# Products of the conditioning vectors with w_mod: steps of two column groups become steps of four

## The chip, the cores and the metric

The kernel runs on one core of a Trainium2 chip. A core has a matrix engine (TensorE, PE in the profile, with its weight loads as PEld), VectorE (DVE), ScalarE (ACT), GpSimd (POOL) and SyncE (SP), which issues this kernel's DMAs. The metric is the device time of one execution in microseconds; the median of several runs counts.

## The reference

One inference step of a two-layer decoder trunk, for a prompt of 1024 positions and 8 samples of 4 positions (1056 rows of width 1024). Layer 0 mixes tokens with sliding-window attention, layer 1 with a gated delta rule. Ahead of each layer the rows are normalised and modulated, and behind it the branch is gated, by vectors made from a conditioning vector c (one for the prompt, eight for the samples):

```python
def modulate(x, c, norm_g, w_mod, b_mod):
    shift, scale, gate = jnp.split(jax.nn.silu(c) @ w_mod + b_mod, 3, axis=-1)
    h = rms_norm(x, norm_g) * (1 + scale[:, None]) + shift[:, None]
    return h, gate[:, None]
...
    for layer in range(DEPTH):
        hp, gp = modulate(xp, c_prompt, norm_g[layer], w_mod[layer], b_mod[layer])
        hs, gs = modulate(xs, c_sample, norm_g[layer], w_mod[layer], b_mod[layer])
...
        xp = xp + gp * op
        xs = xs + gs * osm
```

`w_mod` is 1024 x 3072 float32 for each layer: 1024 columns of shift, 1024 of scale, 1024 of gate. All 9 conditioning vectors go through it at once.

## The kernel before

**The products.** The 9 vectors silu(c), padded to 32, lie transposed in `cT` (128 partitions, 8 row blocks, 32 columns). A product takes one row block k of `cT` as the weights of TensorE (128 x 32) and one piece of `w_mod` (128 rows by 512 columns, 256 KB) as the moving operand. Its output has 32 rows, so it uses a quarter of the array's columns; the first row of its output in the PSUM bank (0, 32, 64 or 96) says which quarter, called a column group here. Eight products, k = 0 to 7, add up to one 512-column piece of the result. Where fewer than four pieces are made in one bank, even and odd k go to different groups and are added later.

**Where they stand.** Shift and scale of layer 0 are made at the start (lines 717 to 743, `modulation_steps`) and stay as they are. Three others are touched:

1. The gate of layer 0: `modulation_gate(0)`, called at line 1218, during the projections of q and v. Two pieces j = 0, 1; step k does two products, to the groups 32 j + 64 (k mod 2). The loads go to the pool `wp`, tag "wr", which has four buffers and which the other weights use too. Loads and steps are put off by `defer(late_p, ticks, fn)` and called by `tick`, which the projections call at the fourth row block of every column group of a q projection (three times) and of every block of v (nine times, t = 0 to 8). `pin` makes the next matmul of the projection wait in program order for the step's last product. At the end VectorE adds rows 0 to 63 of the bank to `modGt`, and ScalarE copies rows 64 to 127.
2. Shift and scale of layer 1: `modulation_rest` (line 1256), beside the attention of layer 0 and its other projections. Four pieces, loaded two at a time into two buffers (tag "wm" of the pool `at`), in 16 steps i of two products each; step i waits until the tick counter of the projections has advanced 20 i (`MM = (0, 20)`), loads its two pieces and waits for them.
3. The gate of layer 1: `modulation_gate(1)`, started at line 1373 in the output projection of layer 0. `pos` counts row blocks of that projection, 16 for a block of 128 rows; step k waits for `pos` to reach 32 + 15 k (`MS`), then does its two products, each when its piece is there, and loads for k + 2, again into "wr". When all is done, `first_weights` (line 1419) loads the first weights of layer 1 into the same four buffers: `cwr`, then two halves that become `kw0h`, `kw0l`, `kw1h`, `kw1l`.

**What sets the order.** Up to line 1287 the Tile scheduler orders the work; engines take their instructions strictly in that order. From there on `Core` is the planner: it keeps a clock for every engine from prices of its own (`issued`, line 111), and generators registered by `weave` yield conditions on these clocks (`ready`, `soon`, `idle`), on ticks or on `pos`. Between two matmuls of the main loop `stages()` runs every generator whose condition holds, the lowest rank in `K` first (`cached` 9, `modulate` 31). What is written so is the program order of every compute engine. The planner prices a float32 product with 32 output rows at 2400 columns per us where its group differs from that of the matmul before it, at 600 otherwise.

Of the kernel before, what the change touches and what calls it, by code (L numbers as in the profile page):

```python
# [5 lines left out]
F32 = mybir.dt.float32  # L6
# [8 lines left out]
P = 128  # L15
D = 1024
KD = D // P
# [202 lines left out]
def body(tc, I, O, cst_ap, dbg=None):  # L220
    nc = tc.nc
# [6 lines left out]
    wp = es.enter_context(tc.tile_pool(name="wp", bufs=1, side="right"))  # L228
# [16 lines left out]
    MS = (32, 15)  # L245
    AH, AI = (a / 10 for a in AM)
    VK = ()
    MM = (0, 20)
# [15 lines left out]
    cT = cp.tile([P, KD, 32], F32, name="cT")  # L264
# [60 lines left out]
    Sc = [cp.tile([P, KD, 9], F32, name=f"Sc{l}") for l in range(2)]  # L325
    modGt = cp.tile([P, 512], F32, name="modG")

    def wmod_tile(l, k, c0):
        wt = wp.tile([P, 512], F32, tag="wr", name="wmod", bufs=4)
        nc.sync.dma_start(wt, I["w_mod"][l, k * P:(k + 1) * P, c0:c0 + 512])  # L330
        return wt

    def modulation(l, load, js=(0, 1)):


        step, end = modulation_steps(l, load, js)
        for k in range(KD):
            step(k)
        return end

    def modulation_steps(l, load, js, pm=None):
        pm = pm or psb("mi")
        nj = len(js)

        def step(k, i=None, q0=0):
            for q, wt in enumerate(load(k if i is None else i)):
                q += q0
                if nj == 1:
                    q += 2 * (k % 2)
                mm = nc.tensor.matmul(pm[32 * q:32 * q + 32, :], cT[:, k, :], wt,  # L350
                                      start=(k <= 2 - nj), stop=(k >= KD - 3 + nj), skip_group_check=True)
            return mm

        return step, lambda: modulation_end(l, js, pm)
# [27 lines left out]
                                           gT[:, l, 4 * j:4 * j + 4].unsqueeze(2).to_broadcast([P, 4, 9]),  # L382
                                           ALU.add, ALU.mult)

    def modulation_gate(l):

        for j in range(2):
            c0 = 2 * D + 512 * j
            nc.sync.dma_start(modGt[32 * j:32 * j + 32], I["b_mod"][l:l + 1, c0:c0 + 512].partition_broadcast(32))
        pg = psb("lg" if l == 0 else "tr")  # L390
        wts = {}

        def load(k):
            wts[k] = [wmod_tile(l, k, 2 * D + j * 512) for j in range(2)]

        def step(k, j):
            r0 = 32 * j + 64 * (k % 2)
            pin[:] = [nc.tensor.matmul(pg[r0:r0 + 32, :], cT[:, k, :], wts[k][j], start=(k < 2), stop=(k >= KD - 2),
                                       skip_group_check=True)]

        def end():
            nc.vector.tensor_tensor(modGt[0:64], modGt[0:64], pg[0:64, :], ALU.add)
            nc.scalar.copy(modGt[64:P], pg[64:P, :])

        if l == 0:
            return load, lambda k: (step(k, 0), step(k, 1)), end

        def steps():
            for k in range(2):
                load(k)  # L410
            for k in range(KD):
                yield lambda: pos[0] >= MS[0] + MS[1] * k
                for j in range(2):
                    yield ready(wts[k][j])
                    step(k, j)
                if k + 2 < KD:
                    load(k + 2)
            yield soon(pg)
            yield idle("vector", modGt)
            end()  # L420

        return steps()
# [42 lines left out]
    late_p, late_c, pin = [], [], []  # L465
# [5 lines left out]
    def defer(late, ticks, fn):  # L471

        late.append([ticks, fn])
# [47 lines left out]
    def ready(*ts):  # L521
        return lambda: plain() or nc.ready(ts) <= nc.free["tensor"]
# [11 lines left out]
    held, pos = {}, [0]  # L534
# [174 lines left out]
    for i, ts in enumerate(xb):  # L709
# [3 lines left out]
        mm = turn_x(ts, dgs, nxt[1])  # L713
# [20 lines left out]
    step, end = modulation_steps(0, lambda k: wm_half[1][k], (1,))  # L734
# [27 lines left out]
    at = at_guard.__enter__()  # L762
    if True:
# [451 lines left out]
        k0 = kproj(0)  # L1215
        q0 = [qproj(0, 0)]
        wv = vproj()
        load, step, end = modulation_gate(0)
        for k in range(KD):
            defer(late_p, k + 1, lambda k=k: load(k))  # L1220
            defer(late_p, k + 3, lambda k=k: step(k))
        defer(late_p, 11, end)
        q0.append(qproj(0, 1))
        hsel = wp.tile([P, P], F32, tag="wr", name="hsel", bufs=4)
        o, w = COFF["hsel"]
# [7 lines left out]
        for t in range(NB + 1):  # L1233
# [3 lines left out]
            for k in range(KD):  # L1237
                hi, lo = wv[k // 2]
                for x, y in ((hhi, hi), (hlo, hi), (hhi, lo)):
                    with pinned():  # L1240
                        mm = nc.tensor.matmul(pv, x[:, k, t * P:t * P + parts], y[:, k % 2, :],
                                              start=(n == 0), stop=(n == 23))
# [12 lines left out]

        def modulation_rest():

            def load(i):
                wts = []
                for j in range(2):  # L1260
                    wt = at.tile([P, 512], F32, tag="wm", name="wm", bufs=2)
                    c0 = (2 * (i % 2) + j) * 512
                    nc.sync.dma_start(wt, I["w_mod"][1, (i // 2) * P:(i // 2 + 1) * P, c0:c0 + 512])
                    wts.append(wt)
                return wts

            pm = yield from bank("tr")
            step, _ = modulation_steps(1, lambda i: wts, (0, 1), pm)
            for i in range(2 * KD):
                yield lambda: ticks[0] >= t0 + MM[0] + MM[1] * i  # L1270
                wts = load(i)
                yield ready(*wts)
                step(i // 2, i, 2 * (i % 2))
            yield soon(pm)
            ma = at.tile([P, 512], F32, tag="wm", name="ma", bufs=2)
# [35 lines left out]
    if True:  # L1311
# [24 lines left out]
        def add_out(pj, i, t, hf):  # L1336

            parts = P if t < NB else TS
            ns = slice(hf * 512, (hf + 1) * 512)
            yield lambda: gathered[0] == 2 * i + hf and i in rows_ and shaped[0] >= i - 1 + hf  # L1340
            xt = rows_[i][0:parts]
            if t < NB:
                yield idle("vector", pj)
                y = x2.tile([P, 512], F32, tag="y", name="y", bufs=2)
                nc.vector.tensor_tensor(y, pj, gate[:, ns], ALU.mult)
                opened.pop(0)
            else:
# [12 lines left out]
                give("lg", pg)  # L1360
            eng = "vector" if i == NB and hf else "gpsimd"
            yield idle(eng, y, xt)
            getattr(nc, eng).tensor_tensor(xt[:, ns], xt[:, ns], y[0:parts], ALU.add)
            if hf == 0:
                rows_["ss", i] = sm.tile([P, 2], F32, tag="ss", name="ss")[0:parts]
            yield soon(xt)
            nc.scalar.activation(y[0:parts], xt[:, ns], AF.Square, accum_out=rows_["ss", i][:, hf:hf + 1])
            gathered[0] += 1
            if hf == 1:
                nc.sync.dma_start(x1d[t * P:t * P + parts], xt)  # L1370
                weave(shape(i, t, xt, rows_["ss", i], parts), "shape")
                if t == NB:
                    weave(modulation_gate(1), "mod")

        def shape(i, t, xt, ss, parts):

# [59 lines left out]
        for i, t in enumerate(turned_):  # L1436
# [7 lines left out]
            for kk, hf in order if i < NB else sorted(order, key=lambda o: o[::-1]):  # L1444
                if True:
                    ns = slice(hf * 512, (hf + 1) * 512)
                    if hf not in pjs:
                        tag = ("pj", "pj", "mi", "mi")[outs[0] % 4]
# [5 lines left out]
                    for k in range(4 * kk, 4 * kk + 4):  # L1454
# [188 lines left out]
    if True:  # L1643
# [534 lines left out]
        pos, prepared, stored, opened, gathered, outs = [0], {}, [0], [], [-1], [0]  # L2178
# [485 lines left out]
    nc = nc.nc  # L2664
# [36 lines left out]
```

## Time and profile before

| | us |
|---|---|
| median of 3 runs (lowest, highest) | 1768.01 (1766.73, 1768.91) |
| the profiled execution | 1762.72 |
| its span, first to last instruction | 1760.8 |

The profile is of one execution, and its view of the busy time by stretch gives for each engine the time in which it worked. "Granted clock" is the share of TensorE's full clock that the throttle let through; its mean was 0.986. In the view by tile, a line "x64: a/b/c, s to t" has the count, the least, median and greatest duration in ns, and the first and last start in us. In the time line a row has start, duration, engine, line, operation, out<-in, shapes and a count of merged instructions; from line 1287 on, all compute instructions are issued by a helper and carry its line, L89.

### The profile page before, as it was taken

How to read it: one execution, taken by the hardware profiler on the slowest of the kernel's cores; microseconds unless marked ns; L12 is line 12 of the kernel's file. 1: busy time of each engine (PE TensorE's matmuls, PEld its weight loads, DVE VectorE, ACT ScalarE, POOL GpSimd, SP SyncE). 2: the span in 40 equal slices, each digit the busy share in tenths (PEclk: the TensorE clock that was granted, in tenths of full speed). 3: DMA queues.
4: the chain of work that ended last, by engine and by line, in shares of the span. 5: the costliest groups of instructions: out<-in, count | busy, mean ns of one | idle time of the engine just before them, and what ended most of it. 6: DMA issues, size and time to landing. Idle time of an engine off the chain costs nothing. (4 is left out here: it accounts for less than half of the span.)

```text
span 1760.8 us, 31819 instructions
## 1 busy us (share of the span) xinstructions
PE 1670.2 (95%) x10666; PEld 1450.0 (82%) x10666; DVE 1214.9 (69%) x3538; ACT 864.3 (49%) x2514; POOL 603.6 (34%) x1170
## 2 busy tenths in 40 slices
PE   6999999999998989799999999999999998998897
PEld 5988888877777889679999999899998987766685
DVE  5426676554555678867878778688697884458677
ACT  5525565453334555156554655564656564433332
POOL 2401110112122234344443544444344445323332
PEclk9999999999999999899999999999999999999999
DMA  9442121233333232132422324224133126764885
GB/s 338 131 112 61 49 69 49 67 103 110 102 108 101 62 88 61 52 87 53 115 61 70 95 62 112 60 67 120 39 94 82 45 76 187 240 193 145 265 258 168
DMA packets 281572, 191.77 MB, mean 109 GB/s; under 512 B 98361, under 2 KB 253881, under 8 KB 281378
## 3 DMA queue, kind: packets, MB, share of 16 engines
q1 hardware_dynamic: 281410, 189.75, 37.5%
q8 instruction: 84, 1.38, 0.3%
q14 instruction: 78, 0.64, 0.1%
HBM read 144.68 MB, written 47.04 MB: 109 GB/s over the span
## 5 line engine op out<-in xcount | busy, mean ns | idle before, releaser
L89 PE MATMUL ps_pj<-h2hi,wl 128*128 128x384 f32 (+1 forms) x1128 | 381.1, 338 | 2.7 <-POOL wl L89 2.5
L89 PE MATMUL ps_pj<-h2lo,wh 128*128 128x384 f32 (+1 forms) x1128 | 381.3, 338 | 0.0
L89 PE MATMUL ps_pj<-h2hi,wh 128*128 128x384 f32 (+1 forms) x1128 | 379.4, 336 | 0.6 <-ACT XR L89 0.6
L89 POOL TENSOR_TENSOR wl<-wr,wh 128x512 fp32r<-128x512 f32 x122 | 164.8, 1352 | 545.7 <-ACT wh L89 518.8
L89 PEld LDWEIGHTS ps_pj<-h2hi,wl 128*128 128x128 f32 x1128 | 213.7, 189 | 6.9 <-POOL wl L89 3.6
L89 PEld LDWEIGHTS ps_pj<-h2hi,wh 128*128 128x128 f32 x1128 | 213.5, 189 | 3.9 <-ACT XR L89 0.9
L89 PEld LDWEIGHTS ps_pj<-h2lo,wh 128*128 128x128 f32 x1128 | 213.6, 189 | 3.7
L89 POOL TENSOR_TENSOR xt<-xt,y 128x512 f32<-128x512 f32 (+1 forms) x48 | 63.3, 1323 | 176.0 <-DVE y L89 137.6
L89 PE MATMUL ps_pj<-hlo,wh 128*128 128x384 f32 (+1 forms) x360 | 119.6, 332 | 0.0
L89 PE MATMUL ps_pj<-hhi,wh 128*128 128x384 f32 (+1 forms) x360 | 118.6, 330 | 0.0
L89 PE MATMUL ps_pj<-hhi,wl 128*128 128x384 f32 (+1 forms) x360 | 118.0, 328 | 0.0
L89 DVE SCALAR_TENSOR_TENSOR vT<-XR,cT,vT 128x384 f32<-128x384 f32 (+1 forms) x144 | 90.3, 640 | 37.9 <-ACT vT L89 36.0
L89 DVE TENSOR_TENSOR tmp<-X 64x31 f32<-64x31 f32 (+15 forms) x248 | 91.2, 368 | 15.5 <-POOL X L89 12.3
L89 DVE TENSOR_TENSOR X<-X,tmp 64x31 f32<-64x31 f32 (+15 forms) x248 | 95.2, 384 | 8.5
L89 ACT CAST wh<-wr 128x512 fp32r<-128x512 f32 x122 | 75.1, 616 | 20.9 <-PE ps_pj L89 15.6
L89 PEld LDWEIGHTS ps_pj<-hlo,wh 128*128 128x128 f32 x360 | 67.8, 188 | 13.6 <-issue 13.5
L89 ACT COPY XR<-ps_pj 128x384 f32<-128x384 f32 (+1 forms) x96 | 43.2, 450 | 68.8 <-PE ps_pj L89 68.6
L89 PEld LDWEIGHTS ps_pj<-hhi,wh 128*128 128x128 f32 x360 | 67.7, 188 | 5.9 <-issue 4.2
L89 ACT ACTIVATE qe<-ps_mi,Eg 128x128 f32<-128x128 f32 x112 | 35.1, 364 | 74.4 <-PE ps_mi L89 74.4
L89 PEld LDWEIGHTS ps_pj<-hhi,wl 128*128 128x128 f32 x360 | 67.8, 188 | 3.3 <-issue 3.3
L89 ACT ACTIVATE prob<-prob,nm 128x256 f32<-128x256 f32 (+1 forms) x128 | 62.3, 489 | 11.3 <-DVE nm L89 11.1
L89 POOL TENSOR_TENSOR rst<-rsw 128x4 f32<-128x4 f32 x96 | 22.6, 235 | 128.7 <-DVE rsw L89 106.0
(580 smaller groups left out, 4330.4 us busy)
## 6 DMA issues: line engine op xcount, KB each, us to landing
wr<-in_gdn_w_in SPq DMA_DIRECT2D x96, 256.0 KB
S<-in_state_gdn_s SPq DMA_DIRECT2D x40, 256.0 KB
xt<-in_x_prompt SPq DMA_DIRECT2D x16, 512.0 KB
wm<-in_w_mod SPq DMA_DIRECT2D x16, 512.0 KB
wr<-in_swa_w_in SPq DMA_DIRECT2D x64, 128.0 KB
wm<-in_w_mod SPq DMA_DIRECT2D x32, 256.0 KB
wmod<-in_w_mod SPq DMA_DIRECT2D x32, 256.0 KB
DP<-gcr SPq DMA_DIRECT2D x64, 128.0 KB
```

What stands on the lines that cost most here:

```text
L89: inst = fn(*args, **kwargs)
```

## The change

`modulation_rest` now loads all four pieces of a row block k at once and does four products in one step, 8 steps instead of 16; step k waits for tick 20 (2 k + 1), and the pieces of k + 1 are loaded right behind step k. `modulation_gate` works on pairs of row blocks m: step m does the products of k = 2 m and 2 m + 1 with both column pieces, four products on the groups 0, 32, 64, 96, 4 steps instead of 8. For layer 0 the loads are called at ticks 1, 1, 4, 7, the steps at 3, 6, 9, 12, the end at 12 (before: loads at 1 to 8, steps at 3 to 10, the end at 11); for layer 1 step m waits for `pos` 32 + 15 (2 m + 1), and the loads of m + 1 follow step m. Buffers: the gate of layer 0 and `modulation_rest` share eight (tag "wg" of `at`), the gate of layer 1 uses the four "wr" of `wp`. The products themselves, their shapes and their number stay.

```diff
     def modulation_steps(l, load, js, pm=None):
...
-        def step(k, i=None, q0=0):
-            for q, wt in enumerate(load(k if i is None else i)):
-                q += q0
+        def step(k):
+            for q, wt in enumerate(load(k)):
                 if nj == 1:
                     q += 2 * (k % 2)
...
-    def modulation_gate(l):
+    def modulation_gate(l, gw, nw, tag):
...
-        def load(k):
-            wts[k] = [wmod_tile(l, k, 2 * D + j * 512) for j in range(2)]
-
-        def step(k, j):
-            r0 = 32 * j + 64 * (k % 2)
-            pin[:] = [nc.tensor.matmul(pg[r0:r0 + 32, :], cT[:, k, :], wts[k][j], start=(k < 2), stop=(k >= KD - 2),
-                                       skip_group_check=True)]
+        def load(m):
+
+            wts[m] = []
+            for k in (2 * m, 2 * m + 1):
+                for j in range(2):
+                    wt = gw.tile([P, 512], F32, tag=tag, name="wmod", bufs=nw)
+                    nc.sync.dma_start(wt, I["w_mod"][l, k * P:(k + 1) * P, 2 * D + j * 512:2 * D + (j + 1) * 512])
+                    wts[m].append(wt)
+
+        def step(m):
+            for q, wt in enumerate(wts.pop(m)):
+                mm = nc.tensor.matmul(pg[32 * q:32 * q + 32, :], cT[:, 2 * m + q // 2, :], wt, start=(m == 0),
+                                      stop=(m == KD // 2 - 1), skip_group_check=True)
+            pin[:] = [mm]
...
         def steps():
-            for k in range(2):
-                load(k)
-            for k in range(KD):
-                yield lambda: pos[0] >= MS[0] + MS[1] * k
-                for j in range(2):
-                    yield ready(wts[k][j])
-                    step(k, j)
-                if k + 2 < KD:
-                    load(k + 2)
+            load(0)
+            for m in range(KD // 2):
+                yield lambda: pos[0] >= MS[0] + MS[1] * (2 * m + 1)
+                yield ready(*wts[m])
+                step(m)
+                if m + 1 < KD // 2:
+                    load(m + 1)
...
-        load, step, end = modulation_gate(0)
-        for k in range(KD):
-            defer(late_p, k + 1, lambda k=k: load(k))
-            defer(late_p, k + 3, lambda k=k: step(k))
-        defer(late_p, 11, end)
+        load, step, end = modulation_gate(0, at, 8, "wg")
+        for m in range(KD // 2):
+            defer(late_p, max(1, 3 * m - 2), lambda m=m: load(m))
+            defer(late_p, 3 * m + 3, lambda m=m: step(m))
+        defer(late_p, 12, end)
...
-            def load(i):
+            def load(k):
                 wts = []
-                for j in range(2):
-                    wt = at.tile([P, 512], F32, tag="wm", name="wm", bufs=2)
-                    c0 = (2 * (i % 2) + j) * 512
-                    nc.sync.dma_start(wt, I["w_mod"][1, (i // 2) * P:(i // 2 + 1) * P, c0:c0 + 512])
+                for j in range(4):
+                    wt = at.tile([P, 512], F32, tag="wg", name="wm", bufs=8)
+                    nc.sync.dma_start(wt, I["w_mod"][1, k * P:(k + 1) * P, j * 512:(j + 1) * 512])
                     wts.append(wt)
                 return wts
...
-            step, _ = modulation_steps(1, lambda i: wts, (0, 1), pm)
-            for i in range(2 * KD):
-                yield lambda: ticks[0] >= t0 + MM[0] + MM[1] * i
-                wts = load(i)
+            step, _ = modulation_steps(1, lambda k: wts, (0, 1), pm)
+            wts = load(0)
+            for k in range(KD):
+                yield lambda: ticks[0] >= t0 + MM[0] + MM[1] * (2 * k + 1)
                 yield ready(*wts)
-                step(i // 2, i, 2 * (i % 2))
+                step(k)
+                if k + 1 < KD:
+                    wts = load(k + 1)
...
-                    weave(modulation_gate(1), "mod")
+                    weave(modulation_gate(1, wp, 4, "wr"), "mod")
```

More of the change, by code (lines that the diff above doesn't have):

```diff
@@ L326, in body @@
     modGt = cp.tile([P, 512], F32, name="modG")
[L328 to L331, printed above, removed]
     def modulation(l, load, js=(0, 1)):
@@ L405, in modulation_gate @@
         if l == 0:
-            return load, lambda k: (step(k, 0), step(k, 1)), end
+            return load, step, end
         def steps():
-            for k in range(2):
-                load(k)
-            for k in range(KD):
-                yield lambda: pos[0] >= MS[0] + MS[1] * k
-                for j in range(2):
-                    yield ready(wts[k][j])
-                    step(k, j)
-                if k + 2 < KD:
-                    load(k + 2)
+            load(0)
[5 more added lines that the diff above has]
+                    load(m + 1)
             yield soon(pg)
@@ L1267, in modulation_rest @@
             pm = yield from bank("tr")
-            step, _ = modulation_steps(1, lambda i: wts, (0, 1), pm)
-            for i in range(2 * KD):
-                yield lambda: ticks[0] >= t0 + MM[0] + MM[1] * i
-                wts = load(i)
+            step, _ = modulation_steps(1, lambda k: wts, (0, 1), pm)
+            wts = load(0)
+            for k in range(KD):
+                yield lambda: ticks[0] >= t0 + MM[0] + MM[1] * (2 * k + 1)
                 yield ready(*wts)
-                step(i // 2, i, 2 * (i % 2))
+                step(k)
+                if k + 1 < KD:
+                    wts = load(k + 1)
             yield soon(pm)
-            ma = at.tile([P, 512], F32, tag="wm", name="ma", bufs=2)
+            ma = at.tile([P, 512], F32, tag="wg", name="ma", bufs=8)
             nc.scalar.copy(ma, pm)
```

## The prediction

> **What bounds the kernel now.** I read the page's engine line first, then busy time by stretch, for the stretches in which the touched products run, then the time line of TensorE around single ones.
>
> ```profile
> PE 1670.2 (95%) x10666; PEld 1450.0 (82%) x10666; DVE 1214.9 (69%) x3538; ACT 864.3 (49%) x2514; POOL 603.6 (34%) x1170
> core 0: us, PE busy (x) PEld busy (x) DVE busy (x) ACT busy (x) POOL busy (x), PEclk, DMA share, GB/s
> 66.00:112.00 46.00, 46.00 (x292) 36.06 (x291) 11.16 (x23) 15.47 (x44) 7.60 (x6) 1.00 0.52 158
> 112.00:375.00 263.00, 262.89 (x1747) 222.81 (x1746) 169.63 (x634) 141.39 (x473) 32.70 (x25) 1.00 0.21 58
> 462.00:545.00 83.00, 83.00 (x401) 63.05 (x396) 47.49 (x144) 29.35 (x67) 16.12 (x12) 1.00 0.38 122
> 545.00:1761.00 1216.00, 1144.17 (x7251) 1018.73 (x7250) 908.38 (x2527) 605.64 (x1793) 497.58 (x1079) 0.98 0.39 109
> ```
>
> The reader is to see three things. PE is busy 95% of the span, so it is the bound. In the three stretches of the touched products (layer 0's gate, layer 1's shift and scale, layer 1's gate) its idle time is 0.00, 0.11 and 0.00 us: a microsecond less of PE there is a microsecond earlier for all that follows. And nobody is close behind: the next engine, VectorE, works 169.63 of 263 us in the longest stretch. Busy PE isn't yet useful PE, though, so the next question is what one interruption by these products costs.
>
> ```profile
> L89 PE MATMUL ps_tr<-wm,cT x64: 592/605/617, 125.6 to 371.6; 128*32 128x512 f32 x64
> L398 PE MATMUL ps_lg<-wmod,cT x32: 592/605/617, 80.9 to 109.6; 128*32 128x512 f32 x32
> L89 PE MATMUL ps_tr<-wmod,cT x32: 592/605/617, 461.6 to 540.6; 128*32 128x512 f32 x32
> ```
>
> These come from the views by tile. Each product in the code is two records: 8 row blocks by 4 column pieces are 32 products of layer 1's shift and scale and 64 records; 8 by 2 are 16 products of each gate and 32 records. The 592 to 617 ns of a record are modelled, and records of one run overlap, so I use distances between starts. "Run" below means products that stand back to back.
>
> ```profile
> 91.90 0.28 PE L1241 MATMUL ps_pj<-wvl,hhi 128*128 128x256 f32 x1
> 92.02 0.28 PE L1241 MATMUL ps_pj<-wvh,hhi 128*128 128x256 f32 x1
> 92.23 1.05 PE L398 MATMUL ps_lg<-wmod,cT 128*32 128x512 f32 x2
> 93.20 0.39 PE L1241 MATMUL ps_pj<-wvh,hlo 128*128 128x256 f32 x1
> 93.43 0.28 PE L1241 MATMUL ps_pj<-wvl,hhi 128*128 128x256 f32 x1
> ...
> 94.66 1.04 PE L398 MATMUL ps_lg<-wmod,cT 128*32 128x512 f32 x2
> ...
> 99.86 1.04 PE L398 MATMUL ps_lg<-wmod,cT 128*32 128x512 f32 x2
> ...
> 101.16 1.04 PE L398 MATMUL ps_lg<-wmod,cT 128*32 128x512 f32 x2
> ```
> ```profile
> 461.56 1.06 PE L89 MATMUL ps_tr<-wmod,cT 128*32 128x512 f32 x6
> 462.55 0.50 PE L89 MATMUL ps_mi<-whi,olo 128*128 128x512 f32 x1
> 462.98 1.04 PE L89 MATMUL ps_tr<-wmod,cT 128*32 128x512 f32 x2
> ...
> 540.16 1.05 PE L89 MATMUL ps_tr<-wmod,cT 128*32 128x512 f32 x4
> 541.14 0.51 PE L89 MATMUL ps_pj<-whi,olo 128*128 128x512 f32 x1
> ```
> ```profile
> 42.45 1.06 PE L350 MATMUL ps_mi<-wm,cT 128*32 128x512 f32 x8
> 43.45 0.45 PE L703 MATMUL ps_pj<-hhi,wh 128*128 128x384 f32 x1
> ```
>
> Columns: start, duration, engine, line, what, count of records. From the start of a run to the next other matmul: one product 93.20 - 92.23 = 0.97 us, two 541.14 - 540.16 = 0.98, three 462.55 - 461.56 = 0.99, four 43.45 - 42.45 = 1.00. **Four products on four column groups cost what one costs, plus 0.01 us for each further one.** The 42.45 row is layer 0's own modulation, steps 5 and 6 with two products each, on groups 2, 3, 0, 1: the arrangement that the change makes everywhere, already in this trace with the same shapes.
>
> A run also slows its neighbours. Matmuls of the v projection start 0.12 us apart (91.90 to 92.02); the one before the run holds 92.23 - 92.02 = 0.21, and the one after it 93.43 - 93.20 = 0.23. That is 0.09 + 0.11 = 0.20 us of edges. So a run of one or two costs 0.98 + 0.20 = 1.18 us of PE, a run of four 1.00 + 0.20 = 1.20.
>
> **The change, part by part.** No product, byte or instruction of the products goes or comes; what changes is how many runs there are.
>
> Layer 1's shift and scale: the 64 records stand in 16 runs of two products (one each 20 ticks of the weave); after, 8 runs of four. 16 x 1.18 - 8 x 1.20 = 9.3 us.
>
> Layer 0's gate: 8 steps of two products, of which two came apart (the one-product rows at 92.23 and 94.66 are one step, 99.86 and 101.16 the other): 6 runs of two and 4 of one, which are 24 + 8 = 32 records. After, 4 runs of four. 10 x 1.18 - 4 x 1.20 = 7.0 us.
>
> Layer 1's gate: 16 products in 8 runs (the three and one at 461.56 and 462.98, then six of two up to 540.16). After, 4 runs: 8 x 1.18 - 4 x 1.20 = 4.6 us.
>
> **Sum: 34 runs become 16, 20.9 us less PE**, all in stretches without PE slack.
>
> What else moves. (a) Loads. Layer 0's gate loads leave the four "wr" buffers for eight of their own and are issued two or three ticks further ahead of most steps (steps at ticks 3, 6, 9, 12; loads at 1, 1, 4, 7). A quad needs four pieces of 256 KB. Behind a late piece PE would stand still, as its matmuls go in order; the scheduler may also part a quad, as it parted two pairs. Bounds: nothing, as in the 46 us without PE idle time and with DMA at 0.52; up to all four quads parted once, 4 x 1.18 = 4.7 us. I take nothing: both parted steps had two ticks of lead, and three of the four quads will have three to five. The last step now falls into the last v block, where VectorE works 11.16 of 46 us, so I cost its later evacuation at nothing. (b) Layer 1's shift and scale: a quad is loaded right after the step before, 40 ticks ahead of its own; eight buffers hold two quads, so SyncE's queue meets buffers that are long free. Nothing. The last step stays at tick 300. (c) Layer 1's gate: a quad takes all four "wr" buffers, and the load of the next waits on SyncE's queue for the quad's last matmul, about 1 us; behind it stand rows of x. Also the last quad holds all four buffers until the end, where before two came free at the step before last:
>
> ```profile
> 529.09 0.73 SPq L89 DMA_DIRECT2D wr<-in_gdn_w_in  x1
> ...
> 541.24 0.38 SPq L89 DMA_DIRECT2D wr<-in_gdn_w_in  x1
> ```
> ```profile
> 542.61 0.62 ACT L89 CAST kw0h<-wr 128x512 fp32r<-128x512 f32 x1
> 543.13 0.63 ACT L89 ACTIVATE y<-xt 128x512 f32<-128x512 f32 x1
> ...
> 544.38 0.62 ACT L89 CAST kw1h<-wr 128x512 fp32r<-128x512 f32 x1 [0.53 <-DMA wr<-in_gdn_w_in]
> ```
> ```profile
> 545.95 0.33 PE L89 MATMUL ps_pj<-h2hi,kw0h 128*128 128x384 f32 x1
> ...
> 551.48 2.07 PE L89 MATMUL ps_lg<-dg,xt 128*128 128x128 f32 x8 [3.78 <-DVE dg L89]
> ```
>
> On this time scale the first weights kw0, so far loaded at 529.09, will be asked for behind the small load cwr at 541.24, so at about 541.7. From issue to cast the second half took 544.38 - 541.24 = 3.14 us, so kw0's cast comes at 544.8 instead of 542.61: before its first use at 545.95, but 2.2 us later in ScalarE's queue, where the square of y at 543.13 stands behind it. That square leads to "dg", for which PE waits 3.78 us at 551.48. Bounds: 0 (the planner puts the square first, PE's 9 early matmuls slip into the wait) to +2.2. I take the middle, **+1.0 us**. (d) The planner prices a product by whether its group differs from the last one's, so two pairs and one quad have the same sum; still, other moments of the weave may order the later work otherwise. The longest single wait of PE after 545 us bounds a wait won or lost:
>
> ```profile
> PE ps_mi L89 <- ACT kb L89: 6.7, 3, 4.6
> ```
>
> So 4.6 us either way (the last column is the longest one); I take nothing.
>
> Sum: -20.9 + 1.0 = -19.9. The profiled execution took 1762.72 us (span 1760.8, 1.9 around it); it becomes 1742.8. The runs' median, 1768.01, is 5.3 above it; the same saving gives **1748 us**.
>
> One page of the Trainium skill speaks against part of this. "TensorE: Matmul & The Clock Gate", section "The cost: per-tile semaphore tail", has each tile that signals its end add some 31 ns (4.7 + 26.3), so two further products would cost 0.06 us a quad and the 16 quads 1.0 us, giving 1749. Here a third product added 0.01 us, so the trace decides.
>
> **The rivals.**
> (1) The saved PE time is taken up by another wait: the weave's attention chains on VectorE and ScalarE arrive no sooner. For: after 545 us PE idles 1216 - 1144.2 = 71.8 us, all on such chains. Against: in the touched stretches there isn't one wait, and VectorE is at 65%. If layer 1's 9.3 us are lost: 1757. If all but 2 us: 1766.
> (2) Layer 0's quads come apart or wait for pieces, +4.7: 1753.
> (3) The change doesn't do what it says: a quad runs as two pairs, 2 x 0.98 + 0.20 = 2.16. Then 34 x 1.18 - 16 x 2.16 = 5.5 us, with the 1.0: 1763. Against: the 42.45 row.
> (4) Four at once slow each other: a single product takes 0.97, and a gain of only three times would give 4 x 0.97 / 3 = 1.29 instead of 1.00, 16 x 0.29 = 4.6 us: 1753. Against: the series 0.97, 0.98, 0.99, 1.00. The same page's section "Measured speedup vs the span model" has 3.07 times for four tiles by rows; four by columns stand here at 3.9.
> (5) Slower: SyncE's queue in layer 1's gate. If the refill of four buffers stands ahead of the row load of x in SyncE's order and SyncE reaches it early, the queue is shut until the quad is done, and the out block behind has no x.
>
> ```profile
> SPq L89 <- PE ps_lg L89: 15.4, 3, 7.3
> ```
>
> SyncE does already wait up to 7.3 us there for PE. A quad's distance is two steps; a step is (540.16 - 462.98) / 6 = 13 us, so a refill could shut the queue for up to 26 us. From 20 us in all over the three refills the gain is gone; three refills of one step, 39 us, with a third hidden by the second row buffer, give 1748 + 26 = 1774. Against: the refill is written right behind its quad, so SyncE should meet it about when the quad ends.
>
> **How the numbers follow.** Forecast (1742 to 1753 with its unknowns) 0.74; (1) 0.05 at 1757 and 0.04 at 1766; (2) 0.08; (3) 0.02; (4) 0.02; (5) 0.03; a better weave, below 1742, 0.02. A measurement here tells about 0.2%, 3.5 us, from no change: above 1771.5 is slower, below 1764.5 faster. So faster 0.93, same 0.04, slower 0.03. The range: 1748 - 4.6 - 1.0 = 1742 below; above, 1748 + 4.7 (2) + 1.2 (rest of kw0) + 4.6 (weave) = 1759. It leaves out (5), (3), the 1766 and the better weave, 0.11.
>
> **What would show it.** Right: the views by tile keep their record counts, in 16 runs of eight records, each about 1.00 us to the next matmul, and the stretch from the first layer 1 product to the last shrinks by about 9 us, the gate's by about 7 and 4.6; PE busy falls by about 20 us. Wrong: runs of four or fewer records (2, 3); gaps ahead of a quad naming a DMA (2, 5); PE idle time after 545 us well above 72 (1); the wait for dg at the end of the out blocks well over 3.8 us (c).

## The result, and the profile after

The median went from 1768.46 us (6 runs, 1766.49 to 1771.61) to **1757.8 us** (6 runs, 1753.06 to 1762.18), a ratio of 0.9936 with a 95% interval of 0.9915 to 0.9957. That is 10.7 us faster, about half of the 19.9 that the prediction's sum gave. The profiled execution of after took 1756.62 us, with a span of 1754.8 and a mean granted clock of 0.981 (0.986 before).

The engine line of the page after, then the touched products in the view by tile:

```profile
PE 1656.2 (94%) x10666; PEld 1451.6 (83%) x10666; DVE 1206.7 (69%) x3538; ACT 863.9 (49%) x2514; POOL 608.5 (35%) x1170
```
```profile
L89 PE MATMUL ps_tr<-wm,cT x64: 592/605/617, 129.8 to 359.4; 128*32 128x512 f32 x64
L398 PE MATMUL ps_lg<-wmod,cT x32: 592/605/617, 80.1 to 116.4; 128*32 128x512 f32 x32
L89 PE MATMUL ps_tr<-wmod,cT x32: 592/604/617, 458.3 to 532.4; 128*32 128x512 f32 x32
```

And two of the new runs in the time line of TensorE (start, duration, engine, line, what, count of records):

```profile
80.14 1.06 PE L398 MATMUL ps_lg<-wmod,cT 128*32 128x512 f32 x8
81.13 0.40 PE L567 MATMUL ps_tr<-hhi,wh 128*128 128x288 f32 x1
...
506.56 1.06 PE L89 MATMUL ps_tr<-wmod,cT 128*32 128x512 f32 x8
507.55 0.50 PE L89 MATMUL ps_pj<-whi,olo 128*128 128x512 f32 x1
```

The counts of records are those of before, 64, 32 and 32, and they stand in 4 + 8 + 4 = 16 runs of eight records. The distance to the next other matmul is 81.13 - 80.14 = 0.99 and 507.55 - 506.56 = 0.99 us; over all 16 runs it is 0.99 or 1.00, in the mean 0.995. So the products became cheaper by what was forecast. PE's busy time fell by only 14.0 us, though, 1670.2 to 1656.2, and the span by 6.0. Something was added elsewhere.

To find it I read when landmarks are reached in the two traces (first or last starts of the view by tile, us):

| | before | after | difference |
|---|---|---|---|
| first product of layer 0's shift and scale (not touched) | 31.9 | 34.0 | +2.1 |
| first attention logits (`ps_lg<-khh,qs`) | 117.4 | 110.1 | -7.3 |
| last product of that attention (`ps_ob<-pT,vsb`) | 377.8 | 374.4 | -3.4 |
| last product of layer 0's projections (`ps_pj<-hhi,wl`) | 422.6 | 408.7 | -13.9 |
| gate rows for the output projection (`ps_lg<-modG,selt`) | 422.9 | 416.2 | -6.7 |
| first weights of layer 1 used (`kw0h`) | 545.9 | 537.7 | -8.2 |

The first row is a late start of this execution, ahead of everything that the change touches (the run with the earlier due moment, below, has 31.9 again). Set against it, the change is worth 2.1 + 7.3 = 9.4 us at the start of the attention, 2.1 + 6.7 = 8.8 at the gate rows and 10.3 at the first weights of layer 1. That last figure is about the 10.7 of the medians; behind it this one pair of executions differs by 2 us more, which is less than the spread of the runs. PE idles 72.5 us behind that landmark, against 71.6 before: the loss is not there, but ahead of it.

Up to the attention the gain is even above the 7.0 of layer 0's gate: 2.4 us of work moved behind that landmark (below). Then 264 us follow in which 8 runs of four replace 16 of two, and the lead does not grow. The projections, which the change lets go ahead, end 13.9 us earlier, but the attention beside them only 3.4. Before, 422.6 - 377.8 = 44.8 us of projections were left when the attention ended. After, 408.7 - 374.4 = 34.3 are left, and what else has to be done then, the attention of the cached samples (`ps_ob<-spT`), no longer fits beside them. The view of busy time by stretch, first before, then after (the second number is the length of the stretch; then the busy time of each engine with its count of instructions, the granted clock, the busy share of the DMA engines and GB/s):

```profile
378.00:416.00 38.00, 34.03 (x388) 29.51 (x387) 17.86 (x49) 16.45 (x42) 9.50 (x11) 0.96 0.48 141
416.00:423.00 7.00, 7.00 (x46) 6.96 (x47) 4.04 (x6) 3.80 (x8) 2.22 (x2) 1.00 0.09 23
423.00:433.00 10.00, 10.00 (x42) 7.59 (x41) 5.18 (x17) 3.24 (x7) 1.91 (x2) 1.00 0.65 175
```
```profile
374.00:408.00 34.00, 30.03 (x338) 26.40 (x335) 15.80 (x40) 13.67 (x34) 7.57 (x9) 1.00 0.50 143
408.00:416.00 8.00, 4.10 (x58) 3.39 (x56) 4.22 (x22) 2.58 (x8) 0.00 (x0) 0.75 0.07 20
416.00:426.00 10.00, 9.76 (x26) 6.50 (x27) 2.27 (x3) 3.78 (x7) 2.98 (x2) 0.68 0.39 120
```

The first row of each has some 4 us of PE idle time; in before a part of it also ran at a lower clock (0.96 in the mean, behind a wait of 2.1 us for `kc`, a piece of the cache). The second row is the difference. Before, PE is busy 7.00 of 7 us there; after, 4.10 of 8, with VectorE at 4.22 and the projections used up. And in the third row PE is busy nearly all the time in both, but after at a granted clock of 0.68, with 26 matmuls in 10 us instead of 42. The time line of TensorE after shows the waits, and the slow matmuls behind them:

```profile
408.68 0.29 PE L89 MATMUL ps_pj<-hhi,wl 128*128 128x288 f32 x1
409.52 0.30 PE L89 MATMUL ps_ob<-spT,vss 128*64 128x32 f32 x2 [0.55 <-DVE spT L89]
...
411.18 0.41 PE L89 MATMUL ps_mi<-cst,sp 128*128 128x128 f32 x2 [0.64 <-DVE sp L89]
...
412.40 0.42 PE L89 MATMUL ps_ob<-spT,vss 128*64 128x32 f32 x2 [0.81 <-DVE spT L89]
...
416.24 3.75 PE L89 MATMUL ps_lg<-modG,selt 128*128 128x512 f32 x4 [2.13 <-issue]
...
421.07 0.63 PE L89 MATMUL ps_pj<-whi,ohi 128*128 128x512 f32 x1
421.50 0.63 PE L89 MATMUL ps_pj<-whi,olo 128*128 128x512 f32 x1
...
422.34 0.40 PE L89 MATMUL ps_pj<-whi,ohi 128*128 128x512 f32 x1
422.57 0.40 PE L89 MATMUL ps_pj<-whi,olo 128*128 128x512 f32 x1
```

After the last projection there is only the chain of the cached samples: VectorE prepares `sp` or `spT`, PE does its small matmuls, VectorE the next. The wait of 2.13 us names no releaser, but what the gate rows need there is `selt`, and SyncE issues its load only behind the last cached product, at 414.13; so this load is most likely the end of the same chain. Before issues it at 415.98, and projections run beside it for 6.7 us. Then the out projection starts at half pace: its matmuls stand 421.50 - 421.07 = 0.43 us apart, and from 422.34 on 0.23. Before, the last cached product started at 415.7, 6.9 us before the projections ended; after, at 413.8, 5.1 us behind their end.

A second, smaller loss stands at the start of the attention. The time line of TensorE after:

```profile
111.28 0.33 PE L89 MATMUL ps_lg<-khh,qs 128*128 128x128 f32 x1 [0.60 <-DVE mx L89]
...
114.38 0.39 PE L89 MATMUL ps_lg<-khh,qs 128*128 128x256 f32 x1 [0.80 <-DVE mx L89]
...
115.92 1.07 PE L398 MATMUL ps_lg<-wmod,cT 128*32 128x512 f32 x8
116.92 0.30 PE L1240 MATMUL ps_tr<-wvh,hhi 128*32 128x256 f32 x1
```

The Tile scheduler put the gate's last step and a piece of the last v block behind the first logits. That is the work that moved. Until the step at 115.92 is done the gate holds its PSUM bank, one of the two that the logits take in turn, so logits wait twice until VectorE has read the maximum (`mx`) of those before: 0.60 + 0.80 = 1.4 us.

### The profile page after: what moved, and what is told of

The parts are those of the page before. It is cut to its first block, busy times and chain, and to the rows that moved or that the text cites. A ratio compares the mean times of both kernels' runs of the same rounds, so it can differ in the third digit from the quotient of the medians.

```text
span 1754.8 us, 31802 instructions
## 1 busy us (share of the span) xinstructions
PE 1656.2 (94%) x10666; PEld 1451.6 (83%) x10666; DVE 1206.7 (69%) x3538; ACT 863.9 (49%) x2514; POOL 608.5 (35%) x1170
## 5 line engine op out<-in xcount | busy, mean ns | idle before, releaser
L89 DVE TENSOR_TENSOR tmp<-X 64x31 f32<-64x31 f32 (+15 forms) x248 | 91.1, 367 | 14.1 <-POOL X L89 10.9
L89 ACT CAST wh<-wr 128x512 fp32r<-128x512 f32 x122 | 75.1, 616 | 18.3 <-PE ps_pj L89 14.1
L89 PEld LDWEIGHTS ps_pj<-hlo,wh 128*128 128x128 f32 x360 | 67.7, 188 | 11.2 <-issue 11.1
```

What stands on the lines that cost most here:

```text
L89: inst = fn(*args, **kwargs)
```

## The experiments

The question is where the other half went. **Theory A**: the products save on the chip what was forecast, and the loss comes from the order that the planner writes. Its clock and its ticks advance otherwise with 8 steps of four than with 16 of two, so attention and projections are laid beside each other differently, the attention ends later against the projections, and the chains at the end lose their cover. The rivals seek the loss in the products themselves or in the other parts of the change, the handover of layer 0's bank among them. The planner's clock is part of the kernel and is read when the kernel is built: its prediction of when TensorE ends. It is no time of the chip, but its difference to before (1438.57 for before, 1449.64 after: +11.1, although it prices the products alike) says what the planner itself thinks of the new order. "Sum" below is: PE time saved by fewer runs (7.0, 9.3, 4.6 from the prediction's working), plus 1.5 for the waits on `mx` where layer 0's gate is changed, plus that difference. For the change it is -20.9 + 1.5 + 11.1 = -8.3, where -10.7 was measured.

Ratios are to the kernel before, run on the same chip in the same series; its medians there were 1767.48, 1768.58 and 1767.97.

### One part alone

Layer 0's gate only: the new `modulation_gate`, here beside the old one under the name `modulation_gate4`, with its loads and steps. The other two keep their steps of two; the pieces of layer 1's shift and scale use the eight buffers "wg" instead of their two.

```diff
-        load, step, end = modulation_gate(0)
+        load, step, end = modulation_gate4(0, at, 8, "wg")
```

> Only layer 0's gate in steps of four; the rest as before. Theory A (the products save what was forecast, and the loss sits in the planner's new order around layer 1's shift and scale): TensorE spends 7.0 us less on the gate's runs (10 runs become 4), about 1.5 to 2 us come back as waits for the second logits bank, and the cached-attention tail looks as before: about 5 us faster, near 1763. Theory B (the loss sits in the buffers and banks of the two gates): 3 us faster at most. Theory C (every saved microsecond of TensorE is half hidden by other engines): 3.5 us faster.

Measured: 1762.03 us (1757.54 to 1770.77), ratio 0.9976 (0.9959 to 0.9994), -5.5 us; the sum is -7.0 + 1.5 = -5.5, since the planner's clock stays as it was. The time line of TensorE has the waits of after again:

```profile
112.02 0.33 PE L89 MATMUL ps_lg<-khh,qs 128*128 128x128 f32 x1 [0.60 <-DVE mx L89]
...
115.11 0.39 PE L89 MATMUL ps_lg<-khh,qs 128*128 128x256 f32 x1 [0.81 <-DVE mx L89]
...
116.66 1.06 PE L443 MATMUL ps_lg<-wmod,cT 128*32 128x512 f32 x8
```

So the 1.4 us belong to this part. That the rest of its 7.0 is gained fits the measured time, whose interval is some 3 us wide to either side, as in the next two.

Layer 1's shift and scale only: the new `modulation_rest`, both gates as before.

```diff
-            for i in range(2 * KD):
-                yield lambda: ticks[0] >= t0 + MM[0] + MM[1] * i
+            for k in range(KD):
+                yield lambda: ticks[0] >= t0 + MM[0] + MM[1] * (2 * k + 1)
```

> Only layer 1's shift and scale in steps of four. Theory A: 9.3 us less on the runs, but the cached attention of the samples is no longer covered by projections at its end (6 us of TensorE idle time and half clock come back, as in the changed kernel): about 3 us faster, near 1765. Theory B: the full 9.3 us, near 1759, and no idle time before the output projection beyond that of the kernel before. Theory C: 4.6 us.

Measured: 1770.53 us (1765.58 to 1774.36), ratio 1.0023 (1.0009 to 1.0038): **3.1 us slower than before**, although it saves the most PE time of the three parts. The planner's clock rose by 11.3, so the sum is -9.3 + 11.3 = +2.0. The gain of 3 us that I expected did not come. The busy time by stretch around the end of the projections:

```profile
380.00:414.00 34.00, 31.91 (x344) 27.97 (x340) 16.57 (x42) 14.46 (x39) 7.65 (x9) 0.95 0.48 143
414.00:421.00 7.00, 2.85 (x51) 2.42 (x51) 4.11 (x18) 1.80 (x5) 0.00 (x0) 0.78 0.14 29
421.00:431.00 10.00, 10.00 (x33) 6.80 (x34) 2.19 (x3) 4.03 (x8) 2.99 (x2) 0.82 0.38 128
```

The hole of after is here with neither gate changed: PE busy 2.85 of 7 us, then 33 matmuls in 10 us at a clock of 0.82. It belongs to this part, but it is not all that this part lost. Counted from the first product of layer 0's shift and scale, `kw0h` comes at 510.8 us here and at 514.0 in before: 3.2 us earlier, as expected, so 6.1 of the 9.3 are lost up to there. In the traces the slower total arises behind it: from `kw0h` to the end this one takes 1226.0 us and that of before 1214.9. How much of that is the order and how much the two executions, 3.6 us above and some 5 below their medians, is not known.

Layer 1's gate only, again by `modulation_gate4`.

```diff
-                    weave(modulation_gate(1), "mod")
+                    weave(modulation_gate4(1, wp, 4, "wr"), "mod")
```

> Only layer 1's gate in steps of four. Theory A: 4.6 us less on the runs, up to 1 us back at the first weights of layer 1: about 4 us faster, near 1764.5. Theory B: the four held buffers cost what is saved: within 2 us of the kernel before. Theory C: 2.3 us.

Measured: 1763.38 us (1758.28 to 1768.79), ratio 0.9979 (0.9963 to 0.9996), -4.1 us; the sum is -4.6 + 1.2 = -3.4. The three parts alone add up to -5.5 + 3.1 - 4.1 = -6.5 us, the whole change gave -10.7. With intervals of some 3 us for each part the 4 us between them are not clear of noise, and by the landmark `kw0h` the parts are 6.4, 3.2 and 3.2 us earlier than before, 12.8 in all, and the whole change 10.3. So it is not shown whether the costs of the orders add.

### The whole change with another order

If only the order is at fault, the same products due at other ticks must give the forecast gain. The steps are due four ticks earlier:

```diff
-    MM = (0, 20)
+    MM = (-4, 20)
```

> The whole change, but layer 1's steps of four are due 4 ticks earlier (MM = (-4, 20) for (0, 20)); products, loads and buffers are the same. By the planner's own clock its attention then ends at tick 324 instead of 343. Theory A: the cached tail is covered again, the idle time of about 8 us between 382 and 418 us falls to about 4, no half clock there: 5 to 7 us faster than the change itself, near 1752. Theories B and C: no difference from the change, 1757 to 1758.

Measured: **1746.7 us** (1742.58 to 1749.66), ratio 0.9888 (0.9870 to 0.9906), -20.8 us, with the planner's clock 0.8 below that of before and a sum of -20.2. This beats both kernels, and it is 11.1 us below the change, where 5 to 7 were expected. The busy time by stretch at the same place:

```profile
363.00:397.00 34.00, 31.99 (x385) 28.05 (x384) 17.82 (x48) 16.24 (x41) 10.30 (x11) 1.00 0.53 158
397.00:406.00 9.00, 9.00 (x57) 9.00 (x58) 5.96 (x8) 4.18 (x8) 2.65 (x2) 1.00 0.23 62
406.00:416.00 10.00, 10.00 (x44) 7.62 (x42) 4.08 (x15) 3.86 (x8) 2.99 (x2) 1.00 0.75 226
```

PE is busy 9.00 of 9 us at the end of the projections, and the out projection runs at full clock, 44 matmuls in its first 10 us. The attention ends at 362.7 and the projections at 406.2, which leaves 43.5 us of them, and the last cached product starts at 396.7, 9.5 us before their end. So a gain of the forecast size was there to be had, and the order decided whether it came. That it comes out at the -20.9 so closely is partly chance: this order keeps the 1.4 us of waits for `mx`, but from the end of the attention to the gate rows PE idles 2.0 us instead of the 4.0 of before, and at full clock.

Was it the due moment alone? Then the kernel before, with its pairs, should also gain from another one. Two tries on before:

```diff
-    MM = (0, 20)
+    MM = (-4, 20)
```

> The kernel before, in steps of two, with MM = (-4, 20). Control: if the earlier due moment were a better order by itself, it should gain here too, about 10 us (1757). If, as theory A has it, it only undoes an unlucky order that the steps of four drew, this kernel gains nothing; by the planner's own clock its end comes 3.3 us later than before: 1767 to 1771.

Measured: 1773.06 us (1769.38 to 1778.51), ratio 1.0024 (1.0011 to 1.0037), 4.5 us slower; the planner's clock said 3.3.

```diff
-    MM = (0, 20)
+    MM = (0, 18)
```

> The kernel before, in steps of two, with MM = (0, 18): no product and no run of products changes, only the moments at which the planner may place them. By the planner's own clock the attention ends at tick 335 instead of 328 and layer 1's gate 5.6 us later. Theory A (the order alone moves microseconds): 4 to 7 us slower than the kernel before, 1772 to 1775. If the order is worth little, within 2 us of 1767.5.

Measured: 1773.7 us (1768.84 to 1778.96), ratio 1.0025 (1.0011 to 1.0040), 5.1 us slower; the planner's clock said 7.0. So of the three moments tried (0, 20) suits the pairs best, and the earlier one gains only together with the steps of four.

Two further orders for the whole change, to see how far the planner's clock tells the chip's time:

```diff
-    MM = (0, 20)
+    MM = (0, 19)
```

> The change with MM = (0, 19), another order of the same work. Its end by the planner's own clock is 1.5 us later than that of the kernel before (the change's own: 11.1 later; with (-4, 20): 0.8 earlier). Theory A, in one sum: the kernel before, less 20.9 us of runs, plus that difference, plus 1.5 us of waits for the logits bank: 18 us faster than the kernel before, near 1750. If (-4, 20) was luck of another kind, about the change's own time, 1757 to 1759.

Measured: 1754.11 us (1750.19 to 1754.97), ratio 0.9921 (0.9905 to 0.9937), -13.9 us. The planner's clock rose by 1.5 only, which gives a sum of -17.9: a miss of 4 us. In the trace the miss lies in layer 1: counted as above, `kw0h` is 18.3 us earlier than before, and from there to the end it takes 1222.2 us against 1214.9 (in an execution of before some 5 us below its median).

```diff
-    MM = (0, 20)
+    MM = (2, 20)
```

> The change with MM = (2, 20). By the planner's own clock it ends 8.5 us later than the kernel before. Theory A by the same sum: 11 us faster than the kernel before, near 1757. If the due moment acts in another way than through the planner's order, nothing ties it to that clock: anywhere from 1746 to 1759.

Measured: 1756.78 us (1756.40 to 1758.24), ratio 0.9939 (0.9924 to 0.9955), -11.2 us; the planner's clock rose by 8.5, the sum is -10.9. The planner's clock tells large losses from small ones, to about 4 us. This order has no hole at the end of the projections: the last cached product starts 5.0 us before their end, and the granted clock from the end of the attention to the gate rows is 1.00. It loses in other places, with PE idle 4.5 us during the attention (before: 0.1), 2.1 up to the gate rows (4.0) and 2.5 up to `kw0h` (1.2). So the uncovered chain is how the change's own order loses, and not the only way in which an order can.

### The handover of layer 0's bank

If the last step comes late because it is due at tick 12, then one tick earlier puts it ahead of the attention. The rival was that the scheduler, which orders this stretch, holds it back for its pieces of `w_mod`.

```diff
-            defer(late_p, 3 * m + 3, lambda m=m: step(m))
-        defer(late_p, 12, end)
+            defer(late_p, min(11, 3 * m + 3), lambda m=m: step(m))
+        defer(late_p, 11, end)
```

> The whole change, but the last step and the end of layer 0's gate come at tick 11 instead of 12, one v block earlier. Theory: the gate's bank of the pair 'lg' is free before the attention starts, so the waits for mx of 0.60 and 0.80 us at 111 and 114 us go and the v projection's last block stands in one piece: 1.4 to 2 us faster than the change, near 1756; the planner's order, and with it the cached tail with its half clock, stays. Rival: the parted v block has nothing to do with the gate's last tick; then both waits stay and the time is that of the change.

Measured: 1759.54 us (1754.72 to 1762.07), ratio 0.9943 (0.9925 to 0.9961), -9.0 us. The step stood at 115.96 as before, and the waits stayed, as the view of waits has it (engine, output and line, what it waited for, us in all, count, longest):

```profile
PE ps_lg L89 <- DVE mx L89: 1.4, 2, 0.8
```

The tick alone was not the cause. The same with the earlier due moment, edited as above in both places:

```diff
-    MM = (0, 20)
+    MM = (-4, 20)
...
-        defer(late_p, 12, end)
+        defer(late_p, 11, end)
```

> The whole change with both edits: layer 1's steps due 4 ticks earlier and layer 0's gate ended at tick 11. Theory: the two gains add, 1.4 to 2 us below the 1746.7 of the due times alone, near 1745. Rival: as for the tick alone, 1746 to 1748.

Measured: 1748.91 us (1744.66 to 1754.43), ratio 0.9885 (0.9865 to 0.9905), -19.7 us: the -20.8 of the due moment, and nothing for the tick. The rival then asks for earlier loads, with the early due moment kept:

```diff
-            defer(late_p, max(1, 3 * m - 2), lambda m=m: load(m))
-            defer(late_p, 3 * m + 3, lambda m=m: step(m))
+            defer(late_p, (1, 1, 3, 5)[m], lambda m=m: load(m))
+            defer(late_p, (2, 4, 8, 12)[m], lambda m=m: step(m))
```

> The change with MM = (-4, 20), and in layer 0's gate the loads at ticks 1, 1, 3, 5 and the steps at 2, 4, 8, 12: the last step's loads have seven ticks of lead instead of five. Theory: the scheduler parts the v projection because it takes the last step's loads to land late; with more lead the last step stands inside the v projection, the logits bank is free when the attention starts, the waits of 0.60 and 0.80 us for mx go: 1.5 to 2 us below 1746.7 to 1748.9, near 1746. Rival: the last step stays behind the start of the attention, the waits stay, 1747 to 1749.

Measured: 1748.5 us (1743.14 to 1752.19), ratio 0.9888 (0.9866 to 0.9910), -19.5 us. The time line of TensorE:

```profile
107.90 0.28 PE L1240 MATMUL ps_tr<-wvl,hhi 128*32 128x256 f32 x1
108.11 1.07 PE L398 MATMUL ps_lg<-wmod,cT 128*32 128x512 f32 x8
109.11 0.30 PE L1240 MATMUL ps_tr<-wvh,hhi 128*32 128x256 f32 x1
```

The last step is back inside the v projection, though it is still due at tick 12, and the two waits are gone. So it is not the tick of the step that decides where it stands. The lead of its loads fits, but the edit moved the earlier steps too, so the lead alone is not shown. In the total the 1.4 us cannot be told: the interval of this kernel and that of the due moment alone are nearly the same, and some 4 us wide to either side. In the two traces `kw0h`, counted as above, comes at 490.0 us here and at 492.1 with the due moment alone.

## Why the prediction was right or wrong, point by point

- **34 runs become 16, 20.9 us less PE: right.** 16 runs of eight records, 0.995 us each to the next matmul. The whole change with the earlier due moment took 20.8 us off, so the saving is not lost by itself. One sign was badly chosen, though: the stretch from the first product to the last also moves with the due moments. It went from 28.7 to 36.3 us for layer 0's gate, from 246.0 to 229.6 for layer 1's shift and scale, from 79.0 to 74.1 for its gate, and measures no saving.
- **Nothing is behind PE in the touched stretches: right before, not after.** The prediction read that PE idle time was 0.11 us in 263, and took it as a property of the work. It was a property of the order, and the order was made anew.
- **(a) Layer 0's gate, loads at nothing, last step at nothing: the cost was 1.4 us.** No quad came apart and none waited for a piece. But the last step slipped behind the first logits, and what that costs is not VectorE's time for the evacuation, which I had looked at, but the bank that stays held until then.
- **(b) Loads of layer 1's shift and scale at nothing: right.** None of its runs has a wait ahead of it that names a DMA.
- **(c) The first weights of layer 1, +1.0: too much.** After, the waits of PE from 530 to 545 us are these:

```profile
PE ps_lg L89 <- DVE dg L89: 1.7, 1, 1.7
...
PE ps_pj L89 <- POOL kw0l L89: 0.2, 1, 0.2
```

  The weights come late by 0.2 us, and the wait for `dg` is 1.7 instead of 3.78. Ahead of it stand 3 early matmuls instead of 9, and it ends 2.90 us behind the first use of `kw0h` instead of 5.53. So nothing was lost here, which is below the lower end of my bounds.
- **(d) Another order of the weave, "I take nothing", bounded by 4.6: this is the step that failed.** The prediction saw that the planner could order the later work otherwise and priced it at nothing because its prices of the products stay the same. But the moments change too: a step of four comes as one block at tick 20 (2 k + 1) and not as two halves 20 ticks apart. The bound was the longest single wait of PE, taken behind 545 us. The loss was not one wait but a row of them with half clock after, at the end of the projections, ahead of 545; by the planner's own clock it came to 11 us. In the two traces it is made up as follows. From the start of the attention to the gate rows the saving of 9.3 is used up by 2.4 to 2.7 us of work moved behind the start, 1.4 of waits for `mx`, some 5.5 of further idle time (1.4 on a wait for `prob` in this stretch that before hasn't, 8.1 instead of 4.0 from the end of the attention to the gate rows) and 0.8 of slow clock. From there to layer 1's first weights the saving of 4.6 is cut by 3.1 of half clock. Against that, before lost about 1.5 us to its own slow clock (0.86 and 0.80 in two stretches of 5 us, shown in the last section), which after has not. -20.9 + 1.4 + 5.5 + 0.8 + 3.1 - 1.5 = -11.6, against the 10.3 of the landmarks; 1.3 us stay open. So (d) cost 7.9 by this sum, more than the 4.6 of its bound.
- **The rivals.** (1), saved time taken up by waits on chains, had the place nearly right, but not the mechanism: those chains did not just fail to come sooner, they lost the work that had covered them, and another due moment brings the saving back. Its 1757 for layer 1's 9.3 us lost agrees with the measured time by chance: the terms above are others. (2) fell, no quad parted. (3) and (4) fell with the 0.995 us. (5) fell: at layer 1's gate PE waited for no piece, and the gate alone gave 4.1 of its 4.6.
- **The semaphore tail** that "TensorE: Matmul & The Clock Gate" of the Trainium skill gives in its section "The cost: per-tile semaphore tail" would, by the prediction's estimate, have made a quad 0.06 us longer than a pair. The 16 quads took 0.995 us to the next matmul against 0.98 for a pair, so such a cost does not show there, as the prediction supposed. In the program as built each product signals in 14 of the 16; in the two where none does, at 99.83 and 324.00 us, the distance is 0.99, against 0.99 or 1.00. When the signals themselves arrive isn't in these rows.

The range of 1742 to 1759 held the time near its upper end, and that was luck: the time lies above the 1742 to 1753 that had the chance of 0.74, and (d) alone went beyond its 4.6. The range held it because the 4.7 us for quads that come apart, which none did, stood in the same sum. Without the 1.0 of (c), and with 1.4 of (a) and 7.9 of (d), the sum is -20.9 + 9.3 = -11.6, and 1768.0 - 11.6 = 1756.4.

What stays open: the planner's clock and the chip differ by up to 4 us from one due moment to another (most with (0, 19), where the trace has it behind `kw0h`), and I did not follow that to a wait.

## What to carry to other kernels

Where a program writes the order of its work by a planner or a scheduler, a change that touches due moments changes the order of everything behind it, and a saving of 20 us can be half given back with the same work: price that by the planner's own end time and by a few neighbouring settings, not by one wait of the old trace. Look at what covers the last chains of a stage (here the projections left when the attention ends, 44.8, 34.3 and 43.5 us) as well as at PE idle time, which can be zero until the cover is too short; with (2, 20) the cover held and PE waited elsewhere. And after such a change set the due moments anew: (0, 20) was the best of three for the pairs and poor for the steps of four, where (-4, 20) gave 1746.7 us.

## What the runs showed of the hardware

**Half clock without a long gap.** At the end of the projections of after, PE had waits of 0.55 to 2.13 us, the longest gap ahead of the gate rows. Two finer stretches of the view of busy time, after:

```profile
411.00:416.00 5.00, 2.11 (x26) 1.75 (x26) 2.17 (x12) 1.40 (x3) 0.00 (x0) 0.61 0.12 32
416.00:421.00 5.00, 4.76 (x7) 2.51 (x8) 0.21 (x1) 1.56 (x3) 0.00 (x0) 0.50 0.48 135
```

PE was busy 2.11 of 5 us in short pieces, and in the 5 us after that, in which it was busy 4.76, it had half the clock: 7 matmuls. The clock fell ahead of the longest wait, when the waits had been 0.55, 0.64 and 0.81 us. The same small product took 0.21 us before the last two of these and 0.27 behind them:

```profile
409.66 0.21 PE L89 MATMUL ps_ob<-spT,vc 128*64 128x16 f32 x1
...
412.64 0.27 PE L89 MATMUL ps_ob<-spT,vc 128*64 128x16 f32 x1
```

Still finer stretches of the view have a clock of 1.00 up to 412.0, of 0.50 from 412.4 and of 0.99 from 422.3 on, so half clock lasted some 10 us. The price of the waits is thus paid once while they last and again behind them. In before, a shorter stretch of slow clock follows the wait of 2.1 us for `kc`:

```profile
386.00:391.00 5.00, 2.92 (x32) 2.18 (x34) 2.58 (x3) 1.45 (x3) 0.92 (x1) 0.86 0.96 255
391.00:396.00 5.00, 5.00 (x81) 4.01 (x74) 3.21 (x8) 3.75 (x9) 1.96 (x2) 0.80 0.36 100
```

In after the clock stayed at 1.00 from 381 to 386 and from 391 to 396, with PE busy 3.01 and 3.18 of 5 us and waits of up to 1.43 and 1.82 us. So the longest wait does not tell the cases apart: 0.81 and 2.1 us lost the clock, 1.43 and 1.82 did not. The busy time in 5 us does so for these four (2.11 and 2.92 against 3.01 and 3.18), but not for a fifth: from 536.5 to 541.5 PE was busy 3.05, and half clock followed. Where the limit lies stays open. The Trainium skill, "TensorE: Matmul & The Clock Gate", section "Why this matters for your kernels", warns of PE-idle gaps over some 3 us; no gap here is that long, and the clock fell all the same. That agrees with the section "A second HAM failure mode: psum-queue depth-cycling" of this page of the Trainium skill, which tells of frequent short idling that makes the clock swing between half and full.

**Four column groups at once are worth nearly four.** Four float32 products of 128 x 32 by 128 x 512 took 0.995 us to the next matmul, one took 0.97, which is 4 x 0.97 / 0.995 = 3.9 times.
